# A two-block model kernel on one core: first table load, first weight split, token mean squares and the banks of three query tiles changed

## The chip, the cores and the metric

The kernel runs on one core of a Trainium2 chip, in one launch. The metric is the device time of that launch in microseconds, the median of several executions. A core has five engines that each work through an instruction list of their own in order: TensorE (PE, with its weight loads shown as PEld), VectorE (DVE), ScalarE (ACT), GpSimd (POOL) and SyncE (SP, which here only issues DMAs). They wait for each other through semaphores.

## The reference, cut to what matters

Two transformer-like blocks run one after the other over 1024 tokens of width 1024. The change lies in the opening of the first block only:

```python
def rms_norm(x, g):
    x32 = x.astype(jnp.float32)
    y = x32 * lax.rsqrt(jnp.mean(x32 * x32, axis=-1, keepdims=True) + EPS)
    return (y * g.astype(jnp.float32)).astype(x.dtype)
...
    h_res = jnp.concatenate([meta_b, x], axis=1)          # 16 meta tokens + 1024 tokens
...
        h = rms_norm(h_res, pre_mix_g[l])
        proj = jnp.einsum('bld,dc->blc', h, w_in[l])
        q1, q2, k1, k2, v, u = jnp.split(
            proj, [QK_COLS, 2 * QK_COLS, 3 * QK_COLS, 4 * QK_COLS, 4 * QK_COLS + V_COLS], axis=-1)
```

`u` then feeds a state-space layer (s5), `q`, `k`, `v` a differential attention with a causal mask. Their outputs are mixed by a projection, a gated feed-forward layer follows, and then the second block (a retention, an RWKV-7 recurrence, another feed-forward layer and a gated embedding) runs in the same manner.

## The kernel before, in words

**Three products for one.** Every large matrix product is made of single-precision values that are rounded to a shorter form (`hi`) with the rest kept (`lo = x - hi`). `mm3` (L146) issues three matmuls per product: hi·hi, hi·lo, lo·hi. ScalarE makes `hi` and VectorE makes `lo`: for weights in `split` (L102, called by `wunit`, L117), for the input in L546 and L547. A weight unit is a 128x1024 tile called `raw`, from which two tiles called `w` come.

**The opening, `project_u` (L503).** The token-wise scale of the norm is not applied to the input. The transposed input `xT` is multiplied by the gain alone (`xh`, `xl`), and 1/rms of a token is applied as the scale of the eviction from PSUM. The work is done in two halves of 512 tokens. For each half the loop over `k` (eight blocks of 128 features) loads a 128x512 piece `xraw` (three buffers), makes `xh` on ScalarE and `xl` on VectorE, and squares the piece on ScalarE (`ssq` for k = 0, `sq` after). GpSimd adds the squares into `ssq` (L553), seven additions for each half. In half 0 each k is at once used for the four token tiles of `u` (12 matmuls of 512 columns per k); w_in comes as four weight units, one for every two k. Between the halves the meta tokens are handled (`um`, 24 matmuls; `msq` their squares). In half 1 each token tile runs through all eight k. So there are 96 + 24 + 96 = 216 matmuls of 512 columns.

The sum of squares over the 128 partitions is a small matmul with a column of ones into the PSUM tile `pss` (L570 for the tokens, L563 for the meta tokens). There is one `pss` bank. VectorE copies `pss` to `ss` (L572); `rsqrt` (L158) on GpSimd makes `xrs`; ScalarE then evicts `u` with that scale (`ue`, L584) and SP stores it (L586). The parameters of the state-space layer (`s5_params`, L899) are computed meanwhile, by many 128x16 operations on VectorE: the tiles named `sp`, `st`, `pw`, `rv` and `f`.

**After it.** `v_all` (L610) and `qk_all(0, ...)` (L662, the keys) make the values and keys from the same `xh`/`xl` with the weights `w_vqk` (128x256 results in PSUM tiles `mm`, two buffers), merged with the state-space layer. Then `qk_all(1, ...)` makes the query tiles, with one `mm` buffer (`MMB=1`), for head pair `hp` 0 in the order t = 0 to 7. After the first 45 steps of it (`QLD`) the attention is merged in, whose scores use two PSUM tiles `sc` of 128x1024 (`SCB=2`). Each tile runs `proj_tile` (L599, 24 matmuls of 256 columns), an eviction on ScalarE (`qk`, L631), a rotation on GpSimd (L641 to L644) and transposes on PE (L650).

**What sets the order.** The program is written as generators that are merged by weights (`merge`, `side`), and a scheduler then places the instructions of each engine, following its own estimate of when each could start. Buffers of a pool are handed out in turn, and an instruction that writes a buffer waits for the last reader of what was there.

Of the kernel before, what the change touches and what calls it, by code (L numbers as in the profile page):

```python
# [12 lines left out]
AF = mybir.ActivationFunctionType  # L13
ALU = mybir.AluOpType
# [42 lines left out]
SCB, TRB, SCW, MMB = 2, 2, 1024, 1  # L57
# [9 lines left out]
class Builder:  # L67
# [46 lines left out]

        return self.pool(name, units, None, stack, side), raws, fine

    def wunit(self, src, ws=None):  # L117
        pw, raws, fine = ws or self.ws
        if not fine:
            raw = self.t(pw, [128, 1024], F32, "raw", raws)  # L120
            ins = self.nc.sync.dma_start(raw, src)
            if self.hold is not None:
                self.after(ins, self.hold)
        hi = self.t(pw, [128, 1024], F32R, "w")
        lo = self.t(pw, [128, 1024], F32R, "w")
        if fine:
            for i in range(2):
                c = slice(512 * i, 512 * i + 512)
                raw = self.t(fine, [128, 512], F32, "raw", raws)
                self.nc.sync.dma_start(raw, src[:, c])  # L130
                self.split(hi[:, c], lo[:, c], raw)
        else:
            self.split(hi, lo, raw)
        return hi, lo
# [368 lines left out]
    def project_u(self, px, between):  # L503

        nc, C, I = self.nc, self.C, self.I
        g = self.C["gcol"]
        self.xT = [[(self.t(px, [128, 512], F32R, f"xh{k}{n}"), self.t(px, [128, 512], F32R, f"xl{k}{n}"))
                    for n in range(2)] for k in range(8)]
        mh = self.t(px, [128, 8, 16], F32R, "mh")
        ml = self.t(px, [128, 8, 16], F32R, "ml")  # L510
        self.mT = (mh, ml)
        with ExitStack() as s2:
            pp = self.pool("pu", 1, stack=s2)
            ps = self.pool("pups", 1, PSUM, s2)
            ssq = self.t(pp, [128, 1024], tag="ssq")
            pu = [self.t(ps, [128, 512], tag="u", bufs=6) for t in range(4)]
            w = []

            def u_mm(o, l, k):
                ww = w[k // 2]  # L520
                wc = slice(512 * (k % 2), 512 * (k % 2) + 512)
                self.mm3(o, l, (ww[0][:, wc], ww[1][:, wc]), k == 0, k == 7)

            for half in range(2):
                hc = slice(512 * half, 512 * half + 512)
                if half:
                    between()
                    for c in ("ident", "rope", "fold", "bones"):
                        self.load_const(c)
                    self.ident = self.C["ident"]  # L530
                    mraw = self.t(pp, [128, 8, 16], tag="mraw")
                    nc.sync.dma_start(mraw, I["mT"])
                    gm = self.t(pp, [128, 8, 16], tag="gm")
                    nc.vector.tensor_tensor(gm, mraw, g[:, 0:8].unsqueeze(2).to_broadcast([128, 8, 16]), ALU.mult)
                    self.split(mh, ml, gm)
                    msq = self.t(pp, [128, 8, 16], tag="msq")
                    nc.scalar.activation(msq, mraw, AF.Square)
                    pu = [self.t(ps, [128, 512], tag="u", bufs=6) for t in range(4)]
                    pm = self.t(ps, [128, 512], tag="um")
                for k in range(8):  # L540
                    raw = self.t(pp, [128, 512], tag="xraw", bufs=3)
                    nc.sync.dma_start(raw, I["xT"][:, k, hc])
                    if half == 0 and k % 2 == 0:
                        w.append(self.wunit(I["w_in"][0, k // 2]))
                    hi, lo = self.xT[k][half]
                    nc.scalar.activation(hi, raw, AF.Copy, scale=g[:, k : k + 1])  # L546
                    nc.vector.scalar_tensor_tensor(lo, raw, g[:, k : k + 1], hi, ALU.mult, ALU.subtract)  # L547
                    if k == 0:
                        nc.scalar.activation(ssq[:, hc], raw, AF.Square)
                    else:  # L550
                        sq = self.t(pp, [128, 512], tag="sq", bufs=2)
                        nc.scalar.activation(sq, raw, AF.Square)
                        nc.gpsimd.tensor_tensor(ssq[:, hc], ssq[:, hc], sq, ALU.add)  # L553
                    if not half:
                        for t in range(4):
                            u_mm(pu[t], self.xl(t, k), k)
                if half:
                    for k in range(8):
                        u_mm(pm[0:16], self.xl(8, k), k)
                pss = self.t(ps, [128, 8], tag="pss")  # L560
                if half:
                    for k in range(8):
                        nc.tensor.matmul(pss[0:16, 4:5], msq[:, k], self.ones, start=k == 0, stop=k == 7)  # L563
                    sm = self.t(pp, [128, 1], tag="ssm")
                    nc.vector.tensor_copy(sm[0:16], pss[0:16, 4:5])
                    self.mrs = self.rsqrt(self.pk, sm, 1024.0, 1e-6, rows=16, tag="mrs")
                    for k in range(8):
                        u_mm(pu[0], self.xl(4, k), k)
                for t in range(4):
                    nc.tensor.matmul(pss[:, t : t + 1], ssq[:, 512 * half + 128 * t : 512 * half + 128 * t + 128], self.ones, start=True, stop=True)  # L570
                ss = self.t(pp, [128, 4], tag=f"ss{half}")
                nc.vector.tensor_copy(ss, pss[:, 0:4])  # L572
                rs = self.rsqrt(self.pk, ss, 1024.0, 1e-6, tag=f"xrs{half}")
                self.xrs.append(rs)
                if half:
                    e = self.t(pp, [128, 512], tag="ue", bufs=2)
                    nc.scalar.activation(e[0:16], pm[0:16], AF.Copy, scale=self.mrs[0:16])
                    self.store("u").dma_start(self.S["um"], e[0:16])
                for t in range(4):
                    if half and t:  # L580
                        for k in range(8):
                            u_mm(pu[t], self.xl(4 + t, k), k)
                    e = self.t(pp, [128, 512], tag="ue", bufs=2)
                    nc.scalar.activation(e, pu[t], AF.Copy, scale=rs[:, t : t + 1])  # L584
                    tt = 4 * half + t
                    self.store("u").dma_start(self.S["u"][128 * tt : 128 * tt + 128], e)  # L586
# [9 lines left out]
    def xscale(self, t):  # L596
        return self.mrs[0:16] if t == 8 else self.xrs[t // 4][:, t % 4 : t % 4 + 1]

    def proj_tile(self, t, w, ps, out):  # L599

        rows = 16 if t == 8 else 128
        p = self.t(ps, [128, 512], tag="mm")[:, 0:256]
        for k in range(8):
            ww = w[k // 4]
            wc = slice(256 * (k % 4), 256 * (k % 4) + 256)
            self.mm3(p[0:rows], self.xl(t, k), (ww[0][:, wc], ww[1][:, wc]), k == 0, k == 7)
            yield
        out.append(p)
# [14 lines left out]
    def qk_tile(self, hp, q, t, w, ps, pq):  # L623

        nc = self.nc
        rows = 16 if t == 8 else 128
        p = []
        yield from self.proj_tile(t, w, ps, p)
        p = p[0]
        e = self.t(pq, [128, 4, 2, 64], tag="qk", bufs=2 if q else QKB)  # L630
        nc.scalar.activation(e[0:rows], p[0:rows].rearrange("p (g d) -> p g d", g=4).unsqueeze(2).to_broadcast([rows, 4, 2, 64]),  # L631
# [6 lines left out]
        ss = tab[:, 1].unsqueeze(1).to_broadcast([rows, 8, 8])  # L638
# [16 lines left out]
        else:  # L655
            c = slice(0, 16) if t == 8 else slice(16 + 128 * t, 144 + 128 * t)
# [1396 lines left out]
    def setup(self):  # L2053
        nc = self.nc
        self.load_const("gcol")
        self.half = self.t(self.const, [128, 16], tag="half")
        nc.gpsimd.memset(self.half, -0.5)
        self.ones = self.t(self.const, [128, 1], tag="ones")
        nc.gpsimd.memset(self.ones, 1.0)

    def run(self):
        self.setup()
# [165 lines left out]
```

## Time and profile before

| | us |
|---|---|
| three runs | 2798.59, 2813.11, 2817.27 |
| median of them | 2813.11 |
| the profiled execution's own time | 2815.24 |
| its span in the profile | 2813.5 |
| what lies around the span | 1.7 |
| PE busy within the span | 2707.0 (96%) |
| PE's first matmul | at 8.84 |
| first matmul of the values | at 71.59 |

The span is the time from the first to the last instruction of the profiled execution. Times in the trace are microseconds from its start. A wait is idle time of an engine in front of an instruction, with the engine or DMA that ended it. The granted clock of TensorE is 1.00 at 2.4 GHz and 0.50 at 1.2 GHz; a stretch in between held some of both.

### The profile page before, as it was taken

The numbers are of one execution on the slowest core, as the hardware profiler recorded it, in microseconds if no ns is written. First come the engines' busy times: TensorE is split into PE (matmuls) and PEld (weight loads), VectorE is DVE, ScalarE is ACT, GpSimd is POOL, SyncE is SP. The second block draws the span as 40 slices with busy tenths as digits, with TensorE's granted clock in tenths as the row PEclk, the third lists the DMA queues.
The fourth block names the chain that finished last, engine by engine and source line by source line (L and its number), as shares of the span: only waits on it lengthen the run. The fifth ranks groups of instructions, "written<-read, shape, count | busy, mean of one in ns | idle before, by whom it ended". The sixth has DMA issues, their size and how long they took to land.

```text
span 2813.5 us, 44349 instructions
## 1 busy us (share of the span) xinstructions
PE 2707.0 (96%) x16624; PEld 2258.4 (80%) x16624; DVE 1763.0 (63%) x3481; ACT 1136.1 (40%) x2210; POOL 627.9 (22%) x1096
## 2 busy tenths in 40 slices
PE   7999998999999999999999999998899999999998
PEld 6988887877888888887787788886787878888887
DVE  6655668377757765464567676766557576665463
ACT  4233566444323344445333333333434233344352
POOL 5024533144111110021132241434031111110010
PEclk9999998999999999999999999999999999999999
DMA  4111020242455566555211111214614555586532
GB/s 144 43 46 48 21 76 23 92 150 90 164 184 175 168 219 236 190 187 188 87 52 43 53 55 47 68 41 135 223 53 135 187 171 170 172 283 204 171 126 85
DMA packets 173807, 352.10 MB, mean 125 GB/s; under 512 B 37784, under 2 KB 83064, under 8 KB 173592
## 3 DMA queue, kind: packets, MB, share of 16 engines
q1 hardware_dynamic: 152248, 277.43, 30.1%
q0 software_dynamic: 21344, 71.84, 7.2%
q8 instruction: 130, 2.13, 0.3%
q14 instruction: 85, 0.70, 0.1%
HBM read 246.90 MB, written 102.30 MB: 124 GB/s over the span
## 4 chain that ended last, share of the span: by engine, by line
PE 68%; issue 11%; DVE 8%; DMA 6%; POOL 3%; ACT 3%; SPq 0%; POOLq 0%; DVEq 0%; ACTq 0%
PE y L149 19%; PE mm L149 15%; PE x L149 7%; PE o L149 6%; PE z L149 5%; PE tr L149 3%; DVE w L104 1%; PE r L1514 1%; PE tr L200 1%; DMA raw<-w_ffn 1%; POOL rp L641 1%; DMA As<-ds 1%; PE o L758 1%; PE u L149 1%; PE r L1604 1%
## 5 line engine op out<-in xcount | busy, mean ns | idle before, releaser
L103 ACT ACTIVATE w<-raw 128x1024 fp32r<-128x1024 f32 (+1 forms) x324 | 286.4, 890 | 418.1 <-PE y L149 147.5
L104 DVE TENSOR_TENSOR w<-raw,w 128x1024 fp32r<-128x1024 f32 (+1 forms) x324 | 331.6, 1028 | 136.3 <-ACT w L103 129.1
L149 PE MATMUL y<-h,w 128*128 128x512 f32 x1152 | 288.6, 392 | 5.4 <-DVE v L353 4.1
L149 PE MATMUL y<-w,h 128*128 128x512 f32 x1152 | 267.3, 391 | 0.0
L149 PE MATMUL mm<-w,h 128*128 128x256 f32 (+1 forms) x1632 | 258.7, 300 | 8.2 <-ACT w L103 7.8
L149 PEld LDWEIGHTS y<-h,w 128*128 128x128 f32 x1152 | 216.5, 189 | 53.1 <-DVE v L353 6.0
L149 PEld LDWEIGHTS y<-w,h 128*128 128x128 f32 x1152 | 215.1, 188 | 44.4 <-ACT mix L1260 0.3
L149 PEld LDWEIGHTS mm<-w,h 128*128 128x128 f32 x1632 | 220.7, 191 | 28.1 <-ACT w L103 8.2
L149 PE MATMUL y<-hx,w 128*128 128x512 f32 x960 | 233.6, 391 | 1.1 <-ACT hx L103 0.9
L149 PEld LDWEIGHTS y<-hx,w 128*128 128x128 f32 x960 | 180.6, 189 | 40.4 <-ACT hx L103 1.8
L149 PE MATMUL mm<-h,w 128*128 128x512 f32 x672 | 188.3, 416 | 6.1 <-ACT w L103 3.0
L104 DVE TENSOR_TENSOR h<-dr,h 128x512 fp32r<-128x512 f32 x154 | 102.3, 687 | 137.5 <-ACT h L103 132.6
L149 PE MATMUL o<-w,h 128*128 128x512 f32 x768 | 182.0, 394 | 2.7 <-DVE mix L1270 1.5
L149 PE MATMUL x<-h,w 128*128 128x512 f32 x672 | 175.3, 392 | 0.0
L149 PEld LDWEIGHTS o<-w,h 128*128 128x128 f32 x768 | 142.5, 188 | 33.1 <-DVE mix L1270 2.2
L103 ACT ACTIVATE h<-dr 128x512 fp32r<-128x512 f32 x154 | 92.6, 624 | 176.3 <-DMA dr<-ff 77.3
L149 PE MATMUL mm<-w,xh 128*128 128x256 f32 x768 | 158.0, 301 | 4.6 <-ACT qk L631 3.4
L149 PEld LDWEIGHTS mm<-h,w 128*128 128x128 f32 x672 | 122.1, 194 | 35.0 <-ACT w L103 4.1
L149 PEld LDWEIGHTS x<-h,w 128*128 128x128 f32 x672 | 124.9, 188 | 26.1 <-ACT w L103 0.9
L149 PE MATMUL z<-h,w 128*128 128x512 f32 x576 | 143.2, 396 | 2.4 <-ACT s L367 1.6
L251 POOL DMA_DIRECT2D ff<-v x66 | 36.4, 551 | 481.6 <-DVE v L361 474.0
L376 DVE TENSOR_TENSOR t<-raw,raw 128x512 f32<-128x512 f32 x40 | 29.8, 744 | 178.0 <-DMA raw<-w_ffn 178.0
(527 smaller groups left out, 5464.8 us busy)
## 6 DMA issues: line engine op xcount, KB each, us to landing
raw<-w_ffn SPq DMA_DIRECT2D x88, 512.0 KB
dr<-ff SPq DMA_DIRECT2D x70, 512.0 KB
ff<-v POOLq DMA_DIRECT2D x88, 256.0 KB, 3.1
td<-w_dn SPq DMA_DIRECT2D x44, 512.0 KB
td<-td POOLq DMA_DIRECT2D x44, 512.0 KB, 3.7
raw<-td SPq DMA_DIRECT2D x40, 512.0 KB
ff<-sd POOLq DMA_DIRECT2D x66, 256.0 KB, 4.8
raw<-w_dn SPq DMA_DIRECT2D x30, 512.0 KB
```

What stands on the lines that cost most here:

```text
L103: self.nc.scalar.activation(hi, src, AF.Copy)
L104: self.nc.vector.tensor_tensor(lo, src, hi, ALU.subtract)
L149: return self.nc.tensor.matmul(*a, **kw, skip_group_check=more)
L200: nc.tensor.transpose(p[:, 128 * j : 128 * j + 128], xs[j][:, 128 * k : 128 * k + 128], self.ident)
L251: self.store("v").dma_start(self.part(("ff", {(0, 0): 0, (1, 0): 1, (1, 1): 2}[m, n]), f // 2), v)
L376: V.tensor_tensor(t[:, lo], r[1][:, lo], r[0][:, lo], ALU.subtract)
L641: nc.gpsimd.tensor_tensor(o, a, b, ALU.mult)
L758: nc.tensor.matmul(po, l, r, start=l is am, stop=False)
L1514: TE.matmul(pa[:, c].rearrange("p m t -> p (m t)"), KB[q, c].rearrange("p m s -> p (m s)"), AR[q, c].rearrange("p m t -> p (m t)"), start= ...
L1604: px = per(lambda o, h, c: TE.matmul(o, E[H[h], c], W[H[h], c], start=True, stop=True))
```

## The change

Four edits, all within the first block. (1) `setup` copies the column of ones to a scrap tile on ScalarE, as the first of ScalarE's instructions. (2) The first unit of w_in is split in two halves of 512 columns. (3) The squares of the transposed pieces and GpSimd's additions go. In their place the input is loaded a second time with tokens on the partitions (`xtok`, 128x1024, two buffers, four tiles for each half), and ScalarE's square sums along the row into `ss`; the ones-matmuls and the copy of `pss` for tokens go too. (4) The query tiles t = 1, 3 and 5 of head pair 0 take an `sc` buffer in place of the `mm` buffer.

```diff
-    def wunit(self, src, ws=None):
+    def wunit(self, src, ws=None, halves=False):
...
+        elif halves:
+            for i in range(2):
+                c = slice(512 * i, 512 * i + 512)
+                self.split(hi[:, c], lo[:, c], raw[:, c])
         else:
             self.split(hi, lo, raw)
...
-            ssq = self.t(pp, [128, 1024], tag="ssq")
...
-                        w.append(self.wunit(I["w_in"][0, k // 2]))
+                        w.append(self.wunit(I["w_in"][0, k // 2], halves=k == 0))
...
-                    if k == 0:
-                        nc.scalar.activation(ssq[:, hc], raw, AF.Square)
-                    else:
-                        sq = self.t(pp, [128, 512], tag="sq", bufs=2)
-                        nc.scalar.activation(sq, raw, AF.Square)
-                        nc.gpsimd.tensor_tensor(ssq[:, hc], ssq[:, hc], sq, ALU.add)
...
-                pss = self.t(ps, [128, 8], tag="pss")
+                ss = self.t(pp, [128, 4], tag=f"ss{half}")
+                for t in range(4):
+                    x = self.t(pp, [128, 1024], tag="xtok", bufs=2)
+                    nc.sync.dma_start(x, I["x"][512 * half + 128 * t : 512 * half + 128 * t + 128])
+                    nc.scalar.activation(x, x, AF.Square, accum_out=ss[:, t : t + 1])
                 if half:
+                    pss = self.t(ps, [128, 8], tag="pss")
...
-                for t in range(4):
-                    nc.tensor.matmul(pss[:, t : t + 1], ssq[:, 512 * half + 128 * t : 512 * half + 128 * t + 128], self.ones, start=True, stop=True)
-                ss = self.t(pp, [128, 4], tag=f"ss{half}")
-                nc.vector.tensor_copy(ss, pss[:, 0:4])
...
-    def proj_tile(self, t, w, ps, out):
+    def proj_tile(self, t, w, ps, out, other=False):
...
-        p = self.t(ps, [128, 512], tag="mm")[:, 0:256]
+        p = (self.t(self.trps, [128, SCW], tag="sc", bufs=SCB) if other else self.t(ps, [128, 512], tag="mm"))[:, 0:256]
...
-        yield from self.proj_tile(t, w, ps, p)
+        yield from self.proj_tile(t, w, ps, p, q and not hp and t in (1, 3, 5))
...
+        nc.scalar.copy(self.t(self.const, [128, 1], tag="warm"), self.ones)
```

The scheduler orders the program anew. ScalarE's list at the start of the kernel, before (xh: rounded input, ssq and sq: squares, w: rounded weights):

```order
L546 ACT_TABLE_LOAD
L546 ACTIVATE xh_40_123<-xraw_168,c_gcol_93 128x512
L549 ACTIVATE ssq_163<-xraw_168 128x512
L103 ACTIVATE w_172<-raw_170 128x1024
L546 ACTIVATE xh_44_127<-xraw_191,c_gcol_93 128x512
L552 ACTIVATE sq_195<-xraw_191 128x512
L546 ACTIVATE xh_48_131<-xraw_210,c_gcol_93 128x512
L552 ACTIVATE sq_220<-xraw_210 128x512
L103 ACTIVATE w_214<-raw_212 128x1024
```

And ScalarE's list at the same place in the changed kernel (warm: the scrap copy, xtok: a tile of the second load):

```order
L2058 ACT_TABLE_LOAD
L2058 COPY warm_99<-ones_97 128x1
L549 ACTIVATE xh_41_125<-xraw_169,c_gcol_93 128x512
L103 ACTIVATE w_173<-raw_171 128x512 x2
L549 ACTIVATE xh_45_129<-xraw_193,c_gcol_93 128x512
L549 ACTIVATE xh_49_133<-xraw_209,c_gcol_93 128x512
L103 ACTIVATE w_213<-raw_211 128x1024
L561 ACTIVATE xtok_324,ss_99_323<-xtok_324 128x1024
L561 ACTIVATE xtok_327,ss_99_323<-xtok_327 128x1024
```

The table load stands in front of the scrap copy, the square between the first input and the first weights is gone, and the first two token squares stand behind the second weight unit, in front of the input of k = 3.

SP's list of DMAs in the changed kernel, from the first weights on (before, the two xtok rows are not there and the order is otherwise nearly the same):

```order
L121 DMA raw_171<-w_in 128x1024
L545 DMA xraw_193<-xT 128x512
L545 DMA xraw_209<-xT 128x512
L121 DMA raw_211<-w_in 128x1024
L560 DMA xtok_324<-x 128x1024
L560 DMA xtok_327<-x 128x1024
L97 DMA c_s5p_352<-s5p 128x48
L545 DMA xraw_231<-xT 128x512
```

Two loads of the second kind stand ahead of the input of k = 3 on the same queue; the other six stand in three more places, each ahead of later pieces of xT.

PE's list where half 0 ends, before (u_167: the last tile of half 0, pss: the bank of the sums, um: the meta tokens):

```order
L149 MATMUL u_167<-w_303,xh_68_151 128x512
L149 MATMUL u_167<-w_302,xl_69_152 128x512
L570 MATMUL pss_342<-ones_97,ssq_163 128x1 x4
L149 MATMUL um_610<-w_172,mh_155 16x512
L149 MATMUL um_610<-w_173,mh_155 16x512
```

And in the changed kernel (u_168 is that last tile there):

```order
L153 MATMUL u_168<-w_290,xh_69_153 128x512
L153 MATMUL u_168<-w_289,xl_70_154 128x512
L153 MATMUL um_597<-w_252,mh_157 16x512
L153 MATMUL um_597<-w_251,ml_158 16x512
L153 MATMUL um_597<-w_251,mh_157 16x512
```

The group into pss for the tokens is gone; the one for the meta tokens, which before was the second into that bank, is now the only one. Of the 24 um matmuls, 13 stand ahead of the last two k of half 0 in the changed kernel, and 11 here.

## Rows read from the trace of the kernel before

**Rows 1.** The page: busy time, share of the span and instructions by engine.

```profile
PE 2707.0 (96%) x16624; PEld 2258.4 (80%) x16624; DVE 1763.0 (63%) x3481; ACT 1136.1 (40%) x2210; POOL 627.9 (22%) x1096
```

**Rows 2.** Windows: from:to, length, busy PE, PEld, DVE, ACT, POOL, PEclk, DMA, GB/s.

```profile
0.00:10.00 10.00, 1.16 (x3) 0.97 (x4) 2.50 (x9) 4.68 (x7) 0.52 (x10) 1.00 0.71 217
10.00:20.00 10.00, 10.00 (x39) 8.06 (x38) 9.90 (x23) 6.93 (x14) 4.76 (x3) 1.00 0.75 263
...
40.00:50.00 10.00, 4.03 (x25) 2.97 (x24) 10.00 (x37) 3.67 (x6) 7.21 (x9) 0.71 0.17 52
50.00:60.00 10.00, 10.00 (x47) 8.33 (x46) 3.91 (x40) 3.30 (x5) 7.73 (x28) 0.95 0.30 110
```

**Rows 3.** Waits from 0 to 120: engine, line, releaser, total us, times, longest.

```profile
PE u L149 <- ACT w L103: 8.8, 1, 8.8
...
PE pss L563 <- DVE ss L572: 6.0, 1, 6.0
```

**Rows 4.** Timeline of the opening: start us, us, engine, line, operation.

```profile
5.31 1.28 ACT L546 ACT_TABLE_LOAD   x1 [5.31 <-DMA xraw<-xT]
6.60 0.72 ACT L546 ACTIVATE xh<-xraw,c_gcol 128x512 fp32r<-128x512 f32 x1
7.23 0.61 ACT L549 ACTIVATE ssq<-xraw 128x512 f32<-128x512 f32 x1
...
7.75 1.04 ACT L103 ACTIVATE w<-raw 128x1024 fp32r<-128x1024 f32 x1
...
8.84 2.50 PE L149 MATMUL u<-w,xh 128*128 128x512 f32 x5 [8.84 <-ACT w L103]
```

**Rows 5.** Timeline between the halves.

```profile
33.93 0.95 PE L570 MATMUL pss<-ones,ssq 128*128 128x1 f32 x8
...
37.12 5.92 POOL L553 TENSOR_TENSOR ssq<-ssq,sq 128x512 f32<-128x512 f32 x4 [4.50 <-ACT sq L552]
...
40.48 1.24 DVE L890 TENSOR_TENSOR st<-sp 128x16 f32<-128x16 f32 x1
...
43.80 0.17 DVE L890 TENSOR_TENSOR st<-sp 128x16 f32<-128x16 f32 x1
...
46.21 0.15 DVE L572 COPY ss<-pss 128x4 f32<-128x4 f32 x1
...
46.41 0.58 PE L563 MATMUL pss<-ones,msq 128*16 128x1 f32 x16 [5.97 <-DVE ss L572]
```

**Rows 6.** Timeline: matmuls of u behind the idle stretch, and the last of them.

```profile
47.95 0.63 PE L149 MATMUL u<-w,xl 128*128 128x512 f32 x1
...
49.23 0.63 PE L149 MATMUL u<-w,xl 128*128 128x512 f32 x1
...
70.69 0.39 PE L149 MATMUL u<-w,xl 128*128 128x512 f32 x1
...
71.37 0.39 PE L149 MATMUL u<-w,xl 128*128 128x512 f32 x1
71.59 0.40 PE L149 MATMUL mm<-w,xh 128*128 128x256 f32 x2
```

**Rows 7.** Windows of 2 us: one in which the DMA queue was full.

```profile
14.00:16.00 2.00, 2.00 (x10) 1.62 (x9) 1.97 (x3) 0.00 (x0) 0.92 (x1) 1.00 0.86 331
```

**Rows 8.** ScalarE's groups by form: a 128x1024 square with a row sum, and reading a sum.

```profile
L187 ACT ACTIVATE nxs<-acc 128x1024 f32<-128x1024 f32 x16 | 16.8, 1052 | 12.4 <-DVE acc L1864 12.1 <-DVE acc L482 0.2
...
L714 ACT ACTIVATION_READ_ACCUMULATOR p<-sc,mx 128x1 f32 x56 | 10.9, 195 | 0.0
```

**Rows 9.** The query tiles: waits over the whole span, one of them, and a window.

```profile
PE mm L149 <- ACT qk L631: 3.4, 5, 0.9
...
283.43 0.80 PE L149 MATMUL mm<-w,xh 128*128 128x256 f32 x2 [0.78 <-ACT qk L631]
...
380.00:390.00 10.00, 10.00 (x80) 9.54 (x79) 6.06 (x14) 4.88 (x17) 3.66 (x10) 1.00 0.21 66
```

**Rows 10.** Windows: where the keys end and the queries begin.

```profile
280.00:290.00 10.00, 8.80 (x49) 8.27 (x50) 2.26 (x6) 1.37 (x2) 2.90 (x10) 0.68 0.17 54
```

## The prediction

> **What bounds the kernel now.** I read the page first: TensorE is busy 96% of the span, no other engine over 63% [rows 1]. So time can only be won where PE idles or runs at its lower clock, and a microsecond saved on another engine counts only if PE waited for it. The windows of the opening came next. PE works 1.16 us of the first ten, and 4.03 of the ten from 40 to 50, at a granted clock of 0.71; from 10 to 20 and from 50 on it is full [rows 2]. The list of waits names both gaps: 8.8 us in front of the first matmul, ended by ScalarE's rounding of the first weights, and 6.0 us in front of `pss` L563, ended by VectorE's copy L572 [rows 3]. The timeline shows why. At the start ScalarE loads its table only when the first input is there, at 5.31, and then rounds the input, squares it and rounds the whole weight unit before PE may begin at 8.84 [rows 4]. Between the halves the token sums were ready soon after 33.93, but the copy that frees the one `pss` bank ran at 46.21, because it stands in VectorE's list behind half 1's `xl` and the small s5 operations; VectorE is full there, 10.00 of 10 [rows 2, 5]. That list is itself slowed: a 128x16 product took 1.24 us while GpSimd's additions ran (37.12 to 43.04), and 0.17 after them [rows 5].
>
> From PE's start at 8.84 to the first matmul of the values at 71.59 it takes 62.75 us [rows 4, 6]. The 216 matmuls of the stage need 49.0 of these at the fast pace: three end 0.68 us apart, 0.227 each [rows 6]. Of the rest 5.97 is the wait [rows 5]. Behind it three matmuls are 1.28 apart, 0.427 each [rows 6]; the two windows hold (0.29 + 0.05) x 2 x 10 = 6.8 us at 1.2 GHz, of which 1.0 is behind 50, so the slow stretch ends near 51 and 4.6 us of work (10.8 matmuls) lost 10.8 x 0.2 = 2.1 us [rows 2]. The first five matmuls were as slow (2.50 us for five) [rows 4], so I put another 2.1 there.
>
> **Edit by edit.** *First table load and first weights.* The load (1.28) moves to where ScalarE only waits, the square (0.61) goes, and half a weight unit is rounded instead of a whole one [rows 4]. If the weights have landed in time, PE starts at 5.31 + 0.72 + 0.62 = 6.65 (a half counted as the 512-column square); if they land only when they were used before, at 7.75, it starts at 8.4. I take 7.4, near the middle: 1.4 us, with bounds 0.4 and 2.2. The scrap copy waits only for a memset and hides in the 5.31 idle microseconds; without that cover it would cost at most the load, 1.28. The second half's rounding and its rest on VectorE lie beside the slow first matmuls.
>
> The Trainium skill (ScalarE: Activation LUTs, What ACT_TABLE_LOAD costs) gives about 2.66 us for a switch of tables, a drain of 1.38 included. The trace differs: from 5.31 to the next instruction at 6.60 there is no room for it [rows 4]. With the page's figure the start could fall by 1.38 more, were it not for the weights.
>
> *Token mean squares.* ScalarE loses 16 squares of 0.61 (9.8 us) [rows 4] and gains eight of 1.05 with a sum read of 0.2 (10.0) [rows 8]: nothing in sum. GpSimd's 14 additions go, about 1.5 us each (5.92 for four) [rows 5]; nothing waits for GpSimd there now, but VectorE gets its pace back. VectorE's copies and PE's 8 token sums go, and with them the second group into `pss`: the wait of 5.97 and the slow stretch behind it (2.1) have no cause left [rows 5]. What is late next? The order lets PE go from half 0 through 11 `um` matmuls into half 1 with nothing to wait for but `xh` and `xl`. So with PE fed, the stage ends at 7.4 + 2.1 (slow start) + 49.0 + 0.5 (the meta sums, 0.58 in [rows 5]) = 59.0.
>
> What may starve it is the second load of the input: 4.2 MB more on SP's queue, in four places ahead of pieces of xT; ScalarE's list stands behind each `xtok` too, and whatever is late there delays `xh`, hence PE. I add up what is ahead of the last piece of xT: xT 4.19 MB, w_in 2.10, x 4.19, three units of w_vqk 1.57, constants 0.35, two stores of u 0.52, 12.9 MB in all. PE needs that piece when it has 6 + 48 matmuls left of the stage (the scheduler runs the first two tiles of half 1 together), at 59.0 - 54 x 0.227 = 46.7, and rounding takes about 1.5 us ahead of that (xh 0.72, and as much for xl). So it must land by 45.2, from 2 us on: 299 GB/s. A full queue moved 331 [rows 7]: it lands at 41, no stall. The first 20 us averaged (217 + 263) / 2 = 240 [rows 2]: it lands at 56, and the stage ends at 56 + 1.5 + 12.3 = 69.7. Before, the queue had holes, since SP waited for input buffers that VectorE freed late; two row-long loads ahead fill them. I take the middle of the two rates, 285: the last piece lands at 47.4 and the stage ends at 61.2. Against 71.6 that is **10.4 us** won, with bounds 1.9 and 13.5 (59.0 with the earlier start of 0.8 more).
>
> The Trainium skill (DMA: Bandwidth & Descriptors, Where 436 GB/s comes from) puts the limit of HBM per core at about 358 GB/s; no row here shows more over ten microseconds. By it 12.9 MB take 36 us, PE does not starve, and the stage would end at 59.0, 2.2 us better than my sum.
>
> What follows (values, keys, state-space layer) starts from the last `u` tile, its stores and the loads behind them on SP; the order there is the same, so I let all of it move up by the 10.4.
>
> *Query tiles in the scores' banks.* With one `mm` buffer each query tile waits for ScalarE to evict the one before: five waits, 3.4 us, the longest 0.9, for instance 0.78 at 283.43 [rows 9]. With every other tile elsewhere, the waits up to t = 6 go, but those of head pair 1 stay, and once the attention is merged in, PE is full (10.00 of 10 [rows 9]) and each borrowed bank is one that scores may need. I take 1.5 us won, with bounds from 2.5 won to 7.2 lost: two tiles (t = 3 and 5) that hold a score bank for 24 matmuls of 0.12 and an eviction of 0.7, 3.6 us each.
>
> *Sum.* 2815.2 - 10.4 - 1.5 = 2803.3 for the profiled execution, which ran 2.1 us over the median of its runs; against that median 2801. From the bounds of its terms the forecast's own range is 2797 to 2818.
>
> **The rivals.** *The wait comes back as a wait for loads* (slower). If the queue moves less than 12.9 / (57.8 - 2) = 231 GB/s, the last piece of xT lands after 57.8, and the stage ends later than the 71.6 of before. For it: the first ten microseconds gave 217 [rows 2], and ScalarE's list couples every piece to an `xtok` ahead of it. Against it: those ten contain the queue's start. At 217 it lands at 61.4, the stage ends at 75.2, 3.6 later: with the queries' 1.5 that is 2.1 slower, 2815 on the median's scale.
>
> *The scores pay for the borrowed banks.* PE is full from there on, so 7.2 us lost come out in full: 2813.1 - 10.4 + 7.2 = 2810. For it: only two score tiles exist and the attention alternates between them. Against: the scheduler knows of the wait and can move other matmuls ahead.
>
> *More is won behind the opening.* The new order also moves key tiles and weight rounding between 160 and 300. There PE idles too, and its clock drops to 0.68 in one window [rows 10]: 6.4 us at half pace, 3.2 lost, and 1.2 idle. If this and the like of it, two more places, go as well, 10 us more: 2791. For it: the weights' rounding stands earlier in VectorE's list at one such place; against: at others the key tiles only change places.
>
> *The change does not do what it says*: VectorE, full as it is, sets the pace of half 1 anyway, so that its last `xl` stays at 48 us. Then PE still has its last 54 matmuls ahead, 12.3 us, and ends at 61: the gain stays. Only together with late loads does it matter, so I give it nothing of its own beyond the first rival.
>
> **How the numbers follow.** Forecast 0.66, late loads 0.10, score banks 0.10, more behind the opening 0.14. A measurement of this kernel can tell about 1%, 28 us, from no change (the three runs lie 19 us apart). None of the cases reaches that by itself; the third with the best bounds of the first two terms comes to 2797 - 10 = 2787, and the spread of the runs may carry it over: 0.08 for faster. Late loads below 150 GB/s, with the slow clock behind each wait, would pass it on the other side: 0.03. Within 1%: 0.89. The range reaches from 2786, the best bounds with the third rival, to 2814, near the late loads.
>
> **What would show it.** Right: the table load before 3 us, PE's first matmul between 6.6 and 8.4, no wait for L572's copy, no ssq on GpSimd, short 128x16 operations throughout, the granted clock at 1.00 from 40 to 60, the values' first matmul near 61, and waits of `mm` for `qk` cut to about 2 us. Wrong: ScalarE idle on DMA `xtok` while PE waits for `xh`; a new idle stretch of PE between 25 and 55; scores waiting for ScalarE's `qk`; or the early gain lost again between 160 and 300, so that the stages there end where they did.

## The result: slower by half a per cent, and the profile after

Six runs of the changed kernel took 2818.1 to 2827.3 us, median 2823.4. Six of the kernel before, the three given ahead among them, took 2798.6 to 2817.3, median 2811.5. The ratio is 1.0052 (95% interval 1.0036 to 1.0069): 14.6 us slower by that ratio, where some 12 us faster was forecast, and the median lies above the end of the range, 2814.

The opening went as forecast or better. The windows of the changed kernel, which answer to [rows 2] (same columns):

```profile
0.00:10.00 10.00, 3.79 (x10) 3.02 (x11) 4.34 (x12) 5.84 (x9) 0.52 (x10) 1.00 0.79 278
10.00:20.00 10.00, 10.00 (x46) 8.25 (x45) 8.04 (x33) 9.04 (x18) 0.00 (x0) 1.00 1.05 388
...
40.00:50.00 10.00, 9.42 (x42) 7.46 (x42) 4.32 (x2) 3.45 (x6) 9.19 (x30) 1.00 0.37 127
50.00:60.00 10.00, 10.00 (x51) 8.52 (x50) 0.00 (x0) 1.38 (x2) 0.00 (x0) 1.00 0.10 36
```

Its timeline, which answers to [rows 4] and to the last row of [rows 6]:

```profile
0.72 1.28 ACT L2058 ACT_TABLE_LOAD   x1 [0.72 <-PEq L2217]
2.01 0.19 ACT L2058 COPY warm<-ones 128x1 f32<-128x1 f32 x1
4.27 0.72 ACT L549 ACTIVATE xh<-xraw,c_gcol 128x512 fp32r<-128x512 f32 x1 [2.06 <-DMA xraw<-xT]
...
5.53 1.15 ACT L103 ACTIVATE w<-raw 128x512 fp32r<-128x512 f32 x2 [0.54 <-DMA raw<-w_in]
...
6.21 2.50 PE L153 MATMUL u<-w,xh 128*128 128x512 f32 x5 [6.21 <-ACT w L103]
...
58.60 0.40 PE L153 MATMUL mm<-w,xh 128*128 128x256 f32 x2
```

PE is no longer empty between 40 and 50, its clock is granted in full up to 60, and the values begin at 58.60, not 71.59. So the time was lost behind the opening, and more than the opening had won. The page shows it as work, not as waiting: PE is busy 2730.5 us where it was 2707.0 [rows 1], with 16 instructions fewer.

```profile
PE 2730.5 (97%) x16608; PEld 2260.8 (80%) x16608; DVE 1750.0 (62%) x3480; ACT 1139.5 (40%) x2212; POOL 608.2 (22%) x1082
```

Two windows of the feed-forward layers, in which PE is full and the clock granted in full, show how. First before, then after (columns as in [rows 2]):

```profile
1100.00:1180.00 80.00, 80.00 (x354) 66.26 (x353) 39.10 (x51) 36.36 (x56) 0.00 (x0) 1.00 0.58 194
2500.00:2600.00 100.00, 100.00 (x442) 82.83 (x442) 55.79 (x76) 40.48 (x59) 6.37 (x12) 1.00 0.72 257
```

```profile
1100.00:1180.00 80.00, 80.00 (x355) 66.26 (x354) 39.32 (x51) 36.40 (x55) 0.00 (x0) 1.00 0.58 197
2500.00:2600.00 100.00, 100.00 (x430) 80.34 (x429) 58.51 (x80) 41.50 (x60) 7.46 (x14) 1.00 0.70 248
```

In the second, 430 matmuls fit where 442 did, with nothing idle and no lower clock; in the first nothing changed. The groups of matmuls from 2000 to 2800, first before and then after (mean ns of one behind the busy time), say which are slower: those that read `h`, not those that read `hx`. In `y<-w,h` the first tile, `w`, is the moving operand, which streams through PE (128x512), and the second, `h`, holds the weights, which are loaded into PE ahead of it (128x128).

```profile
L149 PE MATMUL y<-w,h 128*128 128x512 f32 x528 | 122.3, 391 | 0.0
...
L149 PE MATMUL y<-hx,w 128*128 128x512 f32 x480 | 116.3, 390 | 0.7 <-ACT hx L103 0.5 <-ACT s L367 0.2
```

```profile
L153 PE MATMUL y<-w,h 128*128 128x512 f32 x528 | 125.5, 396 | 0.0
...
L153 PE MATMUL y<-hx,w 128*128 128x512 f32 x480 | 116.4, 390 | 0.5 <-ACT hx L103 0.5
```

Nothing of the change is near these layers but one thing: the scrap tile `warm` of edit 1. Tiles of the constants stand ahead of all others on the left side of SBUF, and a column of one float takes a slot of 32 bytes. In the program `v` stands at byte 18944 of a partition before and at 18976 after, while the tiles that are handed out from the other side (`xh`, one of the two `K`) stay where they were. I had read the diff for instructions and orders, and not for addresses.

### The profile page after: what moved, and what is told of

Same layout as the page of the kernel before. It is cut to its first block, busy times and chain, and to the rows that moved or that the text cites. A ratio compares the mean times of both kernels' runs of the same rounds, so it can differ in the third digit from the quotient of the medians.

```text
span 2825.5 us, 44293 instructions
## 1 busy us (share of the span) xinstructions
PE 2730.5 (97%) x16608; PEld 2260.8 (80%) x16608; DVE 1750.0 (62%) x3480; ACT 1139.5 (40%) x2212; POOL 608.2 (22%) x1082
## 4 chain that ended last, share of the span: by engine, by line
PE 69%; DVE 10%; DMA 8%; issue 8%; ACT 3%; POOL 1%; SPq 1%; POOLq 0%; DVEq 0%; ACTq 0%
PE y L153 20%; PE mm L153 14%; PE x L153 7%; PE o L153 6%; PE z L153 6%; PE tr L153 3%; DMA raw<-w_ffn 2%; DVE w L104 2%; DMA As<-ds 1%; PE tr L204 1%; PE r L1512 1%; PE o L756 1%; PE r L1602 1%; DMA ds<-AA 1%; DMA rkv<-w_o 1%
## 5 line engine op out<-in xcount | busy, mean ns | idle before, releaser
L103 ACT ACTIVATE w<-raw 128x512 fp32r<-128x512 f32 (+1 forms) x325 | 287.0, 889 | 429.9 <-PE y L153 147.1
L104 DVE TENSOR_TENSOR w<-raw,w 128x512 fp32r<-128x512 f32 (+1 forms) x325 | 331.0, 1025 | 142.7 <-ACT w L103 140.3
L153 PEld LDWEIGHTS mm<-w,h 128*128 128x128 f32 x1632 | 224.5, 194 | 30.2 <-ACT w L103 10.1
L153 PE MATMUL mm<-w,xh 128*128 128x256 f32 x720 | 147.9, 301 | 5.2 <-ACT qk L629 2.4
```

Source lines behind the costliest of these rows:

```text
L103: self.nc.scalar.activation(hi, src, AF.Copy)
L104: self.nc.vector.tensor_tensor(lo, src, hi, ALU.subtract)
L153: return self.nc.tensor.matmul(*a, **kw, skip_group_check=more)
```

## Experiments

Ratios are to the kernel before, from runs on the same chip, with 95% intervals.

### First: is it the layout?

`e1`: the changed kernel with a larger scrap tile. `e2`, `e3` and `e4`: the kernel before with an unused tile of 32, 64 or 96 bytes; the order of the instructions is that of before on every engine.

```diff
-        nc.scalar.copy(self.t(self.const, [128, 1], tag="warm"), self.ones)
+        warm = self.t(self.const, [128, 16], tag="warm")       # e1
+        nc.scalar.copy(warm[:, 0:1], self.ones)
...
+        self.t(self.const, [128, 8], tag="pad0")               # e2; e3: 16, e4: 24
```

> The changed kernel with one difference: the scrap tile of the first ScalarE copy takes 64 bytes of a partition in place of 32, so every tile that is laid out behind it on the left side of SBUF moves by 64 bytes against the kernel before and not by 32. The instructions and their order stay as in the changed kernel. Theory 'layout': in the changed kernel 3396 matmuls of 512 columns (kernel before: 120) read a moving operand and weights whose addresses differ by 32 modulo 64; in its trace such a matmul starts the next one 233.3 ns later on the mean, one with equal remainders 227 to 228. With 64 bytes the counts are those of before again, and 3276 x 6.3 ns = 20.6 us go: 2803 us, between 2799 and 2808, below the kernel before (2811.5). No full-pace 512-column matmul of the second block above 230 ns on the mean. Theory 'order': the new order of the keys and queries and the clock behind it cost the time; then nothing changes: 2823 (2818 to 2827).

> The kernel before with one unused tile of 128x8 (32 bytes of a partition) added to the pool of constants, behind the column of ones. Same instructions in the same order. Theory 'layout': 3396 matmuls of 512 columns get operands that differ by 32 modulo 64, as in the changed kernel: 2811.5 + 20.6 = 2832 us, between 2826 and 2836, slower than the changed kernel; the matmuls of the feed-forward layers stand 233 ns apart on the mean. Theory 'order': the layout costs nothing, 2811.5 (2799 to 2817).

> As e2, but the unused tile is 128x16 (64 bytes). Theory 'layout': remainders modulo 64 are those of the kernel before, so 2811.5 (2805 to 2817). If any move of the layout costs (for instance because sizes near the end of SBUF no longer fit as they did, or remainders of 128 count), it is slower by 10 us or more, like e2.

> As e2, but the unused tile is 128x24 (96 bytes). Theory 'layout', remainders modulo 64: like e2, 2832 (2826 to 2836). If the remainder modulo 128 were what counts, e2, e3 and e4 would all be slower than the kernel before. Theory 'order': 2811.5.

Measured: e1 1.0048 (1.0033 to 1.0063), e2 1.0059 (1.0044 to 1.0074), e3 1.0058 (1.0044 to 1.0071), e4 1.0070 (1.0055 to 1.0084). An unused tile that no instruction touches costs as much as the whole change: the theory of the order falls for most of the loss. But my theory that the addresses' remainders modulo 64 count falls with e1 and e3, which should have been fast. The window from 2500 to 2600 in e3, as slow as after:

```profile
2500.00:2600.00 100.00, 100.00 (x430) 81.12 (x429) 53.81 (x71) 40.01 (x57) 5.83 (x11) 1.00 0.68 243
```

### Second: which distance?

`f1` takes the second column of the tile of ones as scrap, so no tile moves. `g0` drops edit 1. `f2` and `f3` are e2 with 128 and 256 bytes.

```diff
-        self.ones = self.t(self.const, [128, 1], tag="ones")
+        o2 = self.t(self.const, [128, 2], tag="ones")           # f1
+        self.ones = o2[:, 0:1]
...
-        nc.scalar.copy(self.t(self.const, [128, 1], tag="warm"), self.ones)
+        nc.scalar.copy(o2[:, 1:2], self.ones)                   # f1; g0: nothing in its place
```

> The changed kernel, whose scrap copy writes into a second column of the tile of ones in place of a tile of its own. That tile fills the same slot as one column did, so every tile behind it stands at the address of the kernel before. Instructions and order are those of the changed kernel. Theory 'distance': a matmul of 512 columns reads its moving operand while the next weights are loaded, and the two get in each other's way unless their addresses are equal modulo some power of two above 64 (all pairs in the runs so far that stand 227 to 228 ns apart are equal modulo 512; those 32, 64, 96, 384, 416, 448 or 480 apart take 231 to 234). In the changed kernel 3160 pairs lost 6.4 ns each, 20.2 us. They go: ratio 1.0052 - 0.0072 = 0.998 of the kernel before (0.996 to 1.000), some 2795 us where that takes 2801. Theory 'order': what costs is the new order, 1.005 as in the changed kernel and with 64 bytes.

> The changed kernel without its first edit: no scrap copy and no scrap tile, so the table load stands at the first input again; the other three edits stay. Theory 'distance': all addresses as in the kernel before, the pairs cost nothing more, the table load costs up to 1.3 us in the opening: ratio 0.9985 (0.9965 to 1.0005), faster than the changed kernel by 18 us although an edit that brings something is gone. Theory 'order': the loss stays, 1.005 to 1.006.

> The kernel before with an unused tile of 128x32 (128 bytes of a partition) in the pool of constants. Some 3430 pairs of a 512-column matmul and the next weights then stand 128 or 384 apart modulo 512. Theory 'distance' with equality modulo 256 or 512: ratio 1.006 to 1.008 (3300 more pairs x 6 ns = 20 us). With equality modulo 128: 1.000.

> As f2 with an unused tile of 128x64 (256 bytes). Some 3320 pairs then stand 256 apart modulo 512. Theory 'distance' with equality modulo 512: ratio 1.006 to 1.008. With equality modulo 256: 1.000 (0.998 to 1.001). If any move of the layout were enough, whatever its size: 1.005 or more.

Measured: f1 0.9993 (0.9981 to 1.0006), g0 0.9988 (0.9977 to 0.9998), f2 1.0051 (1.0032 to 1.0071), f3 0.9996 (0.9985 to 1.0008). A shift of 256 bytes is free, one of 128 is not. The same window in f1 and then in f3:

```profile
2500.00:2600.00 100.00, 100.00 (x443) 82.81 (x442) 54.46 (x72) 40.57 (x58) 5.06 (x10) 1.00 0.71 251
```

```profile
2500.00:2600.00 100.00, 100.00 (x442) 82.81 (x442) 54.70 (x72) 41.97 (x61) 1.58 (x3) 1.00 0.68 239
```

I took ten traces (before, after, e1 to e4, f1 to f3, g2 below), gave every matmul the addresses that its program gives its operands, and grouped those of 512 columns that stand among others of 512 columns at the full clock (220 to 245 ns to the next start) by the distance of the moving operand from the weights of the next matmul (the difference of their addresses in bytes, of which the remainder modulo 256 is kept):

```
distance modulo 256   matmuls   ns to the next start
  0                    50194     227.4
 32                     4284     233.2
 64                     4036     231.3
 96                     2020     233.6
128                     4018     232.9
160                     1125     234.0
192                     2242     233.3
224                     2245     233.4
```

Only zero is fast. Counted without the condition on the neighbours, the kernel before has 144 unequal pairs of 7319, the changed one 3334 of 7347, at 233.3 ns on the mean. At 5.9 ns each (233.3 less the 227.4 of the equal ones), 3190 more make 19 us.

### Third: the edits one by one, at the addresses of before

`g2`: before with edit 3 alone. `g4`: before with edit 4 alone. `g1`: f1 without edit 4. `g5`: f1 without edit 3. Their diffs are the parts of the one shown above.

> The kernel before with the third edit alone: token mean squares from a second load, without the early table load, the split first weights and the borrowed banks. The tiles stand where they stood. Theory 'kept': the wait of 5.97 us between the halves and the slow clock behind it go, the stage of u ends 8 to 9 us earlier and all that follows moves up: ratio 0.997. Theory 'given back': the stage ends 8 to 9 us earlier, but between 180 and 300 us PE then meets weights that are not yet rounded and evictions of query tiles, so that half or more is lost there: ratio 0.9985 to 1.0005.

> The kernel before with the fourth edit alone: query tiles 1, 3 and 5 of head pair 0 in the banks of the scores. Theory 'kept': 1 to 2 us faster, ratio 0.9995. If the borrowed banks cost: 1.001 to 1.0025 (up to 7.2 us). The opening is that of the kernel before, with the wait of 6 us between the halves.

> The changed kernel with the scrap copy in the tile of ones (as f1) and without the fourth edit: the query tiles all use the one mm bank. Theory 'kept': 1.5 us slower than f1, ratio 0.9998. If the borrowed banks cost: faster than f1, 0.997. Theory 'given back': PE waits for the eviction of qk again, but loses no more than the weights make it lose anyway: within 2 us of f1, 0.9986 to 1.0000.

> The changed kernel with the scrap copy in the tile of ones (as f1) and without the third edit: token mean squares by squares of the transposed pieces and GpSimd, as before. Theory 'kept': only 1.4 us of the opening and 1.5 us of the queries are won, ratio 0.999; the wait between the halves is there as before. Theory 'given back': 0.9993 to 1.0003, no different from f1 by more than 3 us, although PE has 8 us less of a lead at 70 us.

Measured: g2 0.9987 (0.9971 to 1.0004), g4 0.9992 (0.9983 to 1.0002), g1 1.0010 (0.9998 to 1.0022), g5 1.0028 (1.0015 to 1.0041). g5 is outside both of its expectations: edits 1, 2 and 4 cost 8 us where edit 4 alone brings 2. Its opening is not to blame (below).

### Fourth: one layer's operand, and the first two edits

`i2`: the unused tile that stands ahead of the first feed-forward layer's tiles made smaller by 32 bytes. `h1`: before with edits 3 and 4. `h2`: h1 with the early table load as in f1.

```diff
-            self.t(self.pool("pad", 1, None, self.pre), [128, 120], tag="pad")
+            self.t(self.pool("pad", 1, None, self.pre), [128, 112], tag="pad")     # i2
```

> The kernel before with one number changed: the unused tile that already stands ahead of the tiles of the first feed-forward layer takes 448 bytes of a partition in place of 480. Only the moving operand of that layer's first products (hx) moves, by 32 bytes; 720 pairs of a 512-column matmul and the next weights then stand 224 apart modulo 256, all others stay equal. Theory 'distance': those 720 take 233.4 ns (as pairs 224 apart did), so y and z of that layer slow down from some 227 to 233 between 610 and 1050 us, the second block keeps 227, and the whole is 4.6 us slower: ratio 1.0016 (1.0005 to 1.003). If the pace hung on where the whole layout stands, and not on the distance of the two operands, nothing is slower: 1.000, 227 everywhere.

> The third and fourth edit alone on the kernel before: token mean squares from a second load, three query tiles in the banks of the scores; table load and first weights as before, all tiles at the addresses of before. If edits 1 and 2 cost more than they bring: the sum of what 3 and 4 brought alone, 0.9987 and 0.9992, that is 0.998 (0.9965 to 0.999), faster than both kernels. If what the edits win early is given back later whatever the edits: 0.999 to 1.0005, like f1 (0.9993) and g0 (0.9988).

> As h1, with the early table load (the scrap copy in the tile of ones): the changed kernel without the split of the first weights and without the move of the layout. If the split is what costs: 0.9975 (0.996 to 0.9985). If the early table load costs (through another order of ScalarE's work): 0.999 or more, slower than h1 by 2 us or more.

Measured: i2 1.0016 (1.0007 to 1.0025), as worked out from 720 pairs. Its matmuls from 640 to 1060, first in the kernel before and then in i2:

```profile
L149 PE MATMUL y<-hx,w 128*128 128x512 f32 x480 | 117.3, 393 | 0.5 <-ACT hx L103 0.5
...
L149 PE MATMUL z<-hx,w 128*128 128x512 f32 x240 | 63.0, 400 | 5.4 <-DVE hx L104 2.2 <-ACT hx L103 2.2 <-DVE w L104 1.0
L149 PE MATMUL z<-h,w 128*128 128x512 f32 x240 | 58.1, 390 | 0.6 <-ACT s L367 0.6
```

```profile
L149 PE MATMUL y<-hx,w 128*128 128x512 f32 x480 | 120.3, 399 | 0.5 <-ACT hx L103 0.5
...
L149 PE MATMUL z<-hx,w 128*128 128x512 f32 x240 | 64.5, 406 | 5.4 <-DVE hx L104 2.2 <-ACT hx L103 2.2 <-DVE w L104 1.0
L149 PE MATMUL z<-h,w 128*128 128x512 f32 x240 | 58.3, 390 | 0.5 <-ACT s L367 0.5
```

Each `hx` matmul is 6 ns longer, the waits are the same to a tenth, and `z<-h,w` beside them did not change. In the second block 443 matmuls fit between 2500 and 2600, as before. So it is the distance between the operands that counts, and not where the whole layout stands.

h1 1.0016 (1.0004 to 1.0028) and h2 1.0021 (1.0009 to 1.0034) are slower, not faster: edits 3 and 4 do not add up, and h2, which lacks the split of the first weights, is slow like g5, so the split is not needed for that. The timelines of single executions, as the starts of the first matmul of each stage (us; `x` is a tile of the first feed-forward layer, `r` one of the second block's mixers; `last rt` is the end of the retention's last matmul):

```
              values  scores  ffn1 x  mixers r  last rt    span   ratio
before          71.6   291.7   604.0    1362.7   2011.8  2813.5
f3 (as before)  70.8   289.2   601.9    1357.5   2002.6  2802.3  0.9996
g4              71.4   286.5   603.3    1361.1   2005.8  2805.2  0.9992
g5              70.0   288.7   608.2    1364.7   2008.7  2809.1  1.0028
g2              61.3   287.6   598.9    1359.6   2003.3  2806.0  0.9987
h1              60.5   284.1   602.8    1360.3   2010.9  2811.9  1.0016
f1              60.9   281.2   592.9    1350.5   2003.1  2806.0  0.9993
g0              58.3   281.1   593.8    1350.7   2001.0  2802.4  0.9988
after           58.6   283.9   594.3    1355.6   2014.5  2825.5  1.0052
```

Against the mean of the first two rows f1 leads by 10.3 at the values, 9.3 at the scores, 10.1 at `x`, 9.6 at `r`, then 4.1 and 1.9. The first two rows, equal but for an unused tile, are themselves 9 us apart at the last `rt`, so a few us in one row mean little. g4, g5, h1 and h2 (not in the table) take 317 to 320 us from the scores to `x`, where the others take 310 to 313, and PE is idle for 20 to 23 us of it in place of 16 to 18. The scheduler wrote orders of the attention for these four that no other kernel has; f1 and after have a new order there too, and it costs nothing. From `r` to the last `rt` the nine kernels whose order of the mixers is that of before or nearly so (before, e2 to e4, f2, f3, g2, g4, i2) take 642 to 650 us, on the mean 645; the eight in which some twenty places of that stage are swapped (after, e1, f1, g0, g1, g5, h1, h2) take 644 to 659, on the mean 652. About five of these seven are waits: PE is idle for 21 to 30 us of the stage in the nine, on the mean 26, and for 27 to 34 in the eight, on the mean 31, while the granted clock is 0.98 in both on the mean. The waits that grow most are those of `mm` for the weights that ScalarE rounds (6.5 to 9.2) and of `rc` for `S` from VectorE (3.2 to 4.6). Whether it is the order alone stays open: these are single executions.

No kernel here is faster than before by more than 0.13%. The only one that is told apart from it on that side is g0, 3.4 us faster than before and some 18 faster than the changed kernel, by leaving edit 1 out.

## Why the prediction was wrong

**The term that failed** is the cheapest of the sum: "The scrap copy waits only for a memset and hides in the 5.31 idle microseconds; without that cover it would cost at most the load, 1.28." The copy does hide: it ran at 2.01 for 0.19. But the tile that it writes moved most of the layout by 32 bytes, which cost 16.6 us (ratio 1.0052 against 0.9993 of f1; 19 us from the count of pairs). The bound was drawn from what the instruction can do on its engine. None of the rivals had an edit act on matmuls that it does not order.

**The opening** was right. The end of the stage of u was put at 61.2; it came at 58.6 (60.9 in f1, 58.3 in g0), at the bound without a stall, 59.0 (57.8 with PE's actual start; PE waited 0.6 for an `xl`). The wait of 5.97 us and the slow clock behind it went, as g2 shows alone: values at 61.3. The middle rate of 285 GB/s was too careful: between 10 and 20 us the queue moved 388. By the Trainium skill (DMA: Bandwidth & Descriptors, Where 436 GB/s comes from) about 358 was the limit; this window is above it, and the measurement decides. PE's first matmul came at 6.21, below the 6.65 that I took as earliest: that sum had the first input at 5.31, and here it was there at 4.27, and ScalarE then waited for the weights until 5.53. Kernels with the opening of before start between 7.4 and 8.8 from one execution to the next, those with edits 1 and 2 between 6.2 and 6.6, so of the 2.6 between the two profiles only some 1.3 are these edits.

**Query tiles.** 1.5 us were forecast. g4 gives 2.2 won (4.8 won to 0.6 lost), f1 against g1 4.8: of that sign and size, though the interval of g4 holds zero, and by f1 and g1 it hangs on the order that comes with it. The waits of `mm` for `qk` fell from 3.4 to 2.4 (1.7 in g4), where about 2 was forecast. A loss of 7.2 by the scores did not come. In g4's execution, though, the stretch from the scores to `x` is some 4 us longer than in the first two rows of the table, and the one ahead of it as much shorter, so that the borrowed banks cost nothing is not shown.

**"I let all of it move up by the 10.4."** That held for half the kernel: f1 still leads by 9.6 at 1350. Then it falls to 4.1 over the mixers and 1.9 at the end, which agrees with its ratio (0.9993, 2.0 us). The step assumed that "the order there is the same" behind the opening; it is not, in the attention and again in the mixers, and in the mixers PE waits some 5 us more. Even with the addresses of before, the forecast would have been 10 us too good.

**Rivals.** Late loads and a loss by the scores did not come. "More is won behind the opening" had the place right and the sign wrong. Where the keys end and the queries begin PE waits for rounded weights and for evictions as it did before, only earlier. In f1, and then in the kernel before:

```profile
268.35 0.38 PE L153 MATMUL mm<-w,xh 128*128 128x256 f32 x1 [1.46 <-ACT w L103]
269.61 0.58 PE L153 MATMUL mm<-w,xh 128*128 128x256 f32 x1 [0.88 <-DVE w L104]
274.18 0.51 PE L153 MATMUL mm<-w,xh 128*128 128x256 f32 x2 [1.26 <-ACT qk L629]
```

```profile
278.08 0.66 PE L650 MATMUL tr<-c_ident,qk 128*128 128x128 f32 x4 [1.65 <-POOL qk L644]
279.94 0.58 PE L149 MATMUL mm<-w,xh 128*128 128x256 f32 x1 [0.87 <-DVE w L104]
```

In some kernels that have the lead the clock is lower around these waits, but not in all. The windows from 180 to 300 of before, after, g2 and f1 (granted clock 0.94, 0.87, 0.87 and 0.93):

```profile
180.00:300.00 120.00, 111.65 (x882) 102.68 (x881) 57.20 (x105) 45.73 (x83) 50.38 (x127) 0.94 0.12 41
```

```profile
180.00:300.00 120.00, 109.30 (x789) 98.71 (x789) 57.24 (x110) 41.86 (x86) 48.52 (x117) 0.87 0.10 33
```

```profile
180.00:300.00 120.00, 108.46 (x783) 97.07 (x781) 55.16 (x105) 39.94 (x81) 46.16 (x112) 0.87 0.09 32
```

```profile
180.00:300.00 120.00, 107.50 (x816) 97.25 (x815) 59.39 (x114) 43.44 (x91) 50.34 (x122) 0.93 0.10 33
```

In g2 the lead shrinks in this stretch from 9.9 us at the values to 2.9 at the scores; the difference in the clock, 0.07 of 120 us, is 8.4. f1 has the same lead, a clock of 0.93, and keeps it (10.3 to 9.3). So the loss in this stretch goes with the clock; why f1 kept the clock and g2 did not is not shown.

## What to carry to other kernels

Read a diff for addresses too: a tile of one float in a pool that lives as long as the kernel moves everything laid out behind it, and a scratch value belongs into a slot that is already there. When a group of matmuls is 2 to 3% slower with PE full, no waits and a full clock, look at its operands' addresses; here the pace stays when the moving operand and the next weights stay equal modulo 256 bytes, as in f1, or with an unused tile of 256 bytes in f3. And a lead won in the opening of a scheduled program is not yet won at its end: take its size at three or four places further on.

## What the runs showed that was not expected

- Matmuls of 512 columns at the full clock stand 227.4 ns apart when the moving operand and the next weights are equal modulo 256 bytes, and 231 to 234 at each of the seven other distances seen (multiples of 32). Of the unequal ones 19,940 differ from both their own and the next weights, 42 from one of the two alone, so which of them counts is not told apart. That the load of weights and the reading of the moving operand get in each other's way is an argument, not shown. The Trainium skill (TensorE: Matmul & The Clock Gate, Step-by-step: what each phase is for) speaks of two independent read ports for the two and says that loading the next weights takes no read bandwidth from the running matmul. It leaves no room for a pace that hangs on the addresses; the runs show one, and decide.
- For matmuls of 256 columns this can't be told: almost all that have unequal next weights belong to the 16 meta tokens, whose weights are narrower.
- The load of ScalarE's table took 1.28 us again, with the next instruction right behind it, and 16 DMA engines moved 388 GB/s over ten microseconds.
